# A second recoded weight tile loaded at the entry of the recurrent layer, and one ring of buffers for two kinds of loads

## The chip, the cores and the metric

The kernel runs on one core of one Trainium2 chip. The metric is device time in microseconds (us) of one execution. A core has five engines with an instruction queue each: PE (TensorE, matrix products; PEld is its loading of weights), DVE (VectorE), ACT (ScalarE), POOL (GpSimd) and SP (SyncE, which here only issues DMAs). Each engine takes its instructions in order, and semaphores make one wait for another.

## What is computed

One inference step of two trunk layers on 640 tokens (512 latent tokens, 128 context tokens), 1024 channels, all in f32. Layer 0 is neighbourhood attention and a SwiGLU feed-forward; layer 1 is a gated linear recurrent unit and a SwiGLU feed-forward. The part of the reference at which the change works is the beginning of layer 1:

```
x  = norm(x) * (1 + scale) + shift              # adaLN, needs a sum of squares over all channels
gate, xr = split(x @ w_in)                      # 1024 -> 2 x 1024
xc = depthwise_conv(xr)                         # width 4
r, i = sigmoid(blockdiag(xc) @ w_a + b_a), sigmoid(blockdiag(xc) @ w_i + b_i)   # for two directions
a  = exp(-8 * r * softplus(-lam));  b = sqrt(1 - a*a) * i * xc
h  = scan(a, b) in both directions;  y = (h_fwd + h_bwd) * gelu(gate);  out = y @ w_out
```

## The kernel before

Activations lie with channels on the 128 partitions and tokens along the free axis, so a 1024 x 1024 weight is 64 blocks of 128 x 128; one "tile" holds the 8 blocks that make 128 output channels (512 KB). An f32 product is made of three products of a faster format: weight and activation are each split in a high part and a low part (`hi`, `lo`), and `chunk` adds hi x hi, hi x lo and lo x hi over the 8 blocks: 24 matmuls for 128 output channels and half the tokens (320 columns, or 322 where two extra columns carry the shift of the modulation). `part` does the same for some of the 8 blocks.

**Weight tiles.** `unit` brings a tile in. It is put in one of two kinds of buffers: kind "m" (`whi`, `wlo`, three buffers each, alive for the whole kernel) or kind "x" (`whx`, `wlx`, buffers of the running phase: two in layer 0's feed-forward, three in the recurrent layer). Without a kind named, the units alternate by a running count (`self.nu`). A tile that comes in raw is split by ACT (high part, L1372) and DVE (low part, L1373). Tiles of the recurrent layer and some later ones are recoded ahead: `keep` (L192 to L203) loads the raw tile on POOL's queue into `kraw` (one buffer), ACT and DVE write both parts into `kw` (one buffer, L200 and L201), and POOL stores the 1 MB result in DRAM (L203); `unit` then loads both parts from there on SP's queue (L187), with no work for ACT or DVE. `keep` is called two or three times behind each gate/up pair in the second and third of the three column groups of layer 0's feed-forward: 29 tiles, 16 of `w_in` first.

**Modulation vectors.** `mod_cols` (L263 to L272) computes SiLU(cond) @ w_mod on DVE: a 512 KB tile on POOL's queue into `mraw` (two buffers), then two multiply-and-sum instructions of 128 x 1024 (L271). They are spread over the attention and layer 0's feed-forward.

**Order of work.** A scheduler places the instructions of attention and the feed-forwards in each engine's queue by its own estimate of time; inside `in_order` the engines PE, DVE and ACT keep the order in which the code is written. The recurrent layer, `lru`, is such a part: a table of steps with a lag (`order`, from L1352 on) is run for t = -1, 0, 1, ..., each step for channel tile t + lag.

**The entry.** `project(..., entry=True)` is the last down-projection of layer 0's feed-forward. Behind it `entry` takes tile KT = 8 of `w_in` (the first of `xr`), computes its product for tokens 320 to 639 into bank `p0`, with the first half of the sum of squares' matmuls (`root`, L453) placed in it, and POOL takes the inverse root (L466). In `lru`, step `whole` makes the diagonal of the inverse root on DVE (`diag`, L470), issues the other half of tile 8's product, and spreads the diagonal over all partitions with PE (`spread`, L474); ACT copies the result (L1228). Then `e1` and `e2` scale the product (DVE, L1242), `c1` and `cv` do the convolution (ACT L1260, DVE L1264), and `gates` are matmuls on it (L1273). Between spread and gates PE has `ga` and `gb`: tile 0 of `w_in` (the first of `gate`), 24 matmuls each.

PSUM has eight banks: three `mm`, and five that the running phase names: in layer 0's feed-forward two `at`, one `rr`, two `mx`, in the recurrent layer one `mx` and two double ones, `gp`.

Of the kernel before, what the change touches and what calls it, by code (L numbers as in the profile page):

```python
# [9 lines left out]
F32 = mybir.dt.float32  # L10
# [5 lines left out]
P = 128  # L16
D = 1024
KT = D // P
# [5 lines left out]
CHB = ((320, 642), (0, 320))  # L24
# [16 lines left out]
KH = KT // 2  # L41
# [81 lines left out]
def _pieces(t0, t1):  # L123
    return [(s, max(a, t0), min(b, t1)) for s, a, b in ((0, 0, NLAT), (1, NLAT, NTOK)) if max(a, t0) < min(b, t1)]


class _Step:
    def __init__(self, ctx, nc, tc, i, o):
        self.ctx, self.nc, self.tc, self.i, self.o = ctx, nc, tc, i, o
        self.main = ctx.enter_context(tc.tile_pool(name="main", bufs=1))  # L130
        self.psum = ctx.enter_context(tc.tile_pool(name="psg", bufs=3, space=bass.MemoryType.PSUM))
        self.n, self.ng, self.nu = 0, 0, 0
        self.anchor, self.pbufs, self.lastq, self.whole = None, {}, {}, False

    def nm(self, s):
        self.n += 1
# [55 lines left out]
    def keep(self, todo, n):  # L192
        nc = self.nc
        for _ in range(min(n, len(todo))):
            name, f = key = todo.pop(0)
            raw = self.t([P, KT, P], F32, "kraw", 1, self.sb)
            nc.gpsimd.dma_start(raw, self.i[name][1, f] if name == "gu" else self.i[name][f])
            w = self.t([P, 2, KT, P], F32R, "kw", 1, self.sb)
            with self.tc.issue_after(self.mark):
                nc.scalar.copy(w[:, 0], raw)  # L200
                nc.vector.tensor_tensor(w[:, 1], raw, w[:, 0].bitcast(F32), ALU.subtract)  # L201
            self.kept[key] = d = self.dram.tile([P, 2 * D], F32, tag=f"k{name}{f}", name=f"k{name}{f}")
            nc.gpsimd.dma_start(d, w.rearrange("p h k m -> p (h k m)").bitcast(F32))  # L203
# [59 lines left out]
    def mod_cols(self, l, j, out):  # L263
        nc = self.nc
        for f in range(KT):
            w = self.t([P, D], F32, "mraw", 2, self.sb)
            nc.gpsimd.dma_start(w, self.i["wm"][l * 6 + j - 2, f])  # L267
            for s in range(2):
                prod = self.t([P, D], F32, "mprod", 1, self.sb)
                with self.tc.issue_after(self.anchor) if self.anchor else nullcontext():  # L270
                    nc.vector.scalar_tensor_tensor(prod, w, 1.0, self.csb[:, s], ALU.mult, ALU.mult, accum_out=out[:, s, f:f + 1])  # L271
            yield  # L272
        nc.vector.tensor_tensor(out, out, self.col(f"bm{l}{j}").unsqueeze(1).broadcast_to([P, 2, KT]), ALU.add)
# [221 lines left out]
        return self.stat_spread(self.stat_diag(self.stat_root(t0, t1, newton)))  # L495

    def entry(self, hi, lo):
        self.u0, self.p0 = self.unit(("wi", KT), "m"), self.pg(False)
        t0, t1 = CHB[0]
        ps = self.p0[:, 0:t1 - t0]  # L500
        with self.in_order(ORDERED[:1]):
            self.part(ps, self.u0, hi, lo, range(KT - 1), t0, t1)
            self.rs = self.root(range(0, NTOK, P), [(self.ssq, 0)])
            self.part(ps, self.u0, hi, lo, (KT - 1,), t0, t1)
# [27 lines left out]
    def project(self, w, hi, lo, gk, nxt=None, done=None, ahead=False, entry=False):  # L532
        G = self.need(self.gcols, gk)
        self.whole = entry
        for f in range(KT):
            u = self.unit(w[f], "m" if ahead else None)
            for t0, t1 in CH:
                self.residual(f, t0, t1, self.chunk(u, hi, lo, t0, t1, not ahead or f > 1), G, nxt)
                if nxt:
                    self.scale(f, t0, t1, *nxt)  # L540
            if done:
                done(f)
        if entry:
            self.shift(*nxt)
            self.entry(*nxt[1:])
        elif nxt:
            self.stats()
            self.shift(*nxt)
        self.whole = False
# [489 lines left out]
    def s_sums(self, q):  # L1039
        nc, g = self.nc, q["g"]  # L1040
        q["u"], src = self.t([P, KT, P], F32, "raw", 3), q["u"]
        nc.sync.dma_start(q["u"], src)
        ss = q["S"] = [self.t([P, KT, P], F32, "sum", 2, self.sb) for _ in range(2)]
        s1, s2, s3, s4 = [s[:, a:a + KH] for s in ss for a in (0, KH)]
        g1, g2, u1, u2 = [t[:, a:a + KH] for t in (g, q["u"]) for a in (0, KH)]
        ops = (s1, u1, u2, ALU.add), (s2, s1, g1, ALU.subtract), (s3, g1, u1, ALU.subtract), (s4, g2, s2, ALU.subtract)

        def run(two):
            def go(vector):
                for o in two:  # L1050
                    (nc.vector if vector else nc.gpsimd).tensor_tensor(*o)
            return go
        return run(ops[:2]), run(ops[2:])
# [7 lines left out]
    def sum_weights(self, q):  # L1061
        with self.tc.issue_after(self.pw):
            for run in self.s_sums(q):
                run(False)
        for i in range(2):
            self.s_split(q, i)
# [133 lines left out]
    def lru(self, hi, lo, yhi, ylo, lp):  # L1200
        nc = self.nc
        Z = [{} for _ in range(KT)]

        def tile(shape, tag, bufs):
            return self.t(shape, F32, tag, bufs, lp)
# [13 lines left out]
        def whole(f, z):  # L1219
            if f == 0:  # L1220
                dg = tile([P, NT, P], "gl", 3)
                self.diag(dg, self.rs, NT)
                z["pb"] = self.chunk(z["u"], hi, lo, *CHB[1], False)
                ps = self.pp.tile([P, 1024], F32, tag="gp", name=self.nm("gp"), bufs=2)
                self.spread(dg, range(0, NTOK, P), ps, 0)
                self.rt = self.t([P, NTOK], F32, "r", 1)
                for _, a, b in _pieces(0, NTOK):
                    nc.scalar.copy(self.rt[:, a:b], ps[:, a:b])  # L1228
# [102 lines left out]

        def ga(f, z):
            z["g"] = tile([P, NTOK], "gl", 3)
            z["v"] = self.unit(("wi", f), "x")
            z["pg"] = self.chunk(z["v"], hi, lo, *CHB[0], False)

        def gb(f, z):
            z["ph"] = self.chunk(z["v"], hi, lo, *CHB[1], False)
# [20 lines left out]
        def ls(f, z):  # L1359
            nc.vector.tensor_tensor(ylo[:, f], z["y"], yhi[:, f].bitcast(F32), ALU.subtract)  # L1360

        g, h, e, d = [[fn(n) for n in range(k)] for fn, k in ((gates, 4), (tanhs, 4), (exps, 2), (halves, 2))]
        order = ((g[0], 0), (h[0], 0), (g[1], 0), (h[1], 0), (cl, 0), (e[0], 0), (e[1], 0), (g[2], 0), (xa, 1), (whole, 1), (g[3], 0), (d[0], 0),
                 (h[2], 0), (sc, -1), (su, -1), (e1, 1), (xb, 1), (pad, 1), (h[3], 0), (d[1], 0), (yg, -1), (e2, 1), (egb, 0), (c1, 1),
                 (sq, 0), (ti, 0), (hs, -1), (ga, 1), (cv, 1), (s1, 0), (bg, 1), (ls, -1), (gb, 1), (ega, 1), (ge, 0), (mu, 0))
        for t in range(-1, KT + 1):
            for step, lag in order:
# [27 lines left out]
    def run(self):  # L1395
# [63 lines left out]
            nc.sync.dma_start(o["nv"], V[:, 4])  # L1459
        xhi = self.big(n=NTOK + 2)  # L1460
        xlo = self.big(n=NTOK + 2)
        self.new_x(xpool)
        self.load_x(i["x"])
        xd = dram.tile([D, NTOK], F32, tag="xd", name="xd")
# [45 lines left out]
```

## Time and profile before

| | |
|---|---|
| runs | 1536.15, 1536.77, 1539.8 us (median 1536.77) |
| the profiled execution | 1532.3 us, of which 1530.5 us lie between its first and its last instruction |
| attention, with the start | 0 to about 350 us |
| layer 0, feed-forward with the projection before it | about 350 to 858 us |
| recurrent layer | about 858 to 1020 us |
| its output projection and layer 1's feed-forward | about 1020 to 1530 us |

In the listings, a row of the timeline has the start in us, the time in us, engine, line, operation, tile written <- tiles read, shapes and count; where the engine stood idle ahead of it, brackets give how long and what ended that. Rows of the stages have start and end, length, then busy us and instructions of each engine, the granted PE clock (1.00 is full), the busy share of the 16 DMA engines and GB/s. Matmuls overlap in the records: one of 320 columns is listed with 0.31 us, and the next starts 0.15 us later.

### The profile page before, as it was taken

What the parts mean: (1) busy time and instruction counts of PE and PEld (TensorE: products, weight loads), DVE (VectorE), ACT (ScalarE), POOL (GpSimd) and SP (SyncE); (2) the same over time, 40 slices, a digit from 0 to 9 for tenths busy, and PEclk for the clock granted to TensorE, in tenths of its full rate; (3) what the DMA queues carried; (4) which work ended last, traced back from release to release, by engine and by line L of the source; (5) the groups of instructions that cost most, each with busy time, mean ns of one, the idle gap of its engine ahead of it and who ended that gap; (6) DMA issues with size and microseconds to landing.
All of it is one profiled execution on the core that took longest, in us unless ns stands there. A gap on an engine that the chain in (4) does not pass through costs nothing.

```text
span 1530.5 us, 26161 instructions
## 1 busy us (share of the span) xinstructions
PE 1478.7 (97%) x10295; PEld 1433.8 (94%) x10295; DVE 1075.5 (70%) x2044; ACT 716.9 (47%) x1312; POOL 261.7 (17%) x319
## 2 busy tenths in 40 slices
PE   6999999989999999999999799999999999999997
PEld 4899999879999999999999788889989999999996
DVE  5678788969999997555556368884876666555646
ACT  4676666664333123423344277873644342424342
POOL 2101122100111111110011001112122323232210
PEclk9999999999999999999999899999999999999998
DMA  9545656535566668667668734237333231313111
GB/s 378 165 115 157 182 165 173 149 142 193 179 205 182 202 211 273 210 234 239 222 237 285 279 126 131 88 111 267 112 118 97 69 111 56 111 56 104 62 55 70
DMA packets 80779, 249.61 MB, mean 163 GB/s; under 512 B 9072, under 2 KB 22544, under 8 KB 76816
## 3 DMA queue, kind: packets, MB, share of 16 engines
q1 hardware_dynamic: 59696, 157.59, 31.6%
q0 software_dynamic: 20672, 90.20, 17.9%
q8 instruction: 81, 1.33, 0.3%
q14 instruction: 42, 0.34, 0.1%
q10 hardware_dynamic: 288, 0.16, 0.0%
HBM read 202.02 MB, written 39.33 MB: 158 GB/s over the span
## 4 chain that ended last, share of the span: by engine, by line
PE 88%; DVE 4%; DMA 3%; ACT 2%; issue 1%; POOL 1%; SPq 0%; DVEq 0%; POOLq 0%; ACTq 0%
PE mm L233 13%; PE mm L235 13%; PE mm L234 13%; PE mx L233 5%; PE mx L235 5%; PE mx L234 5%; PE mx L1078 3%; PE mx L1079 3%; PE mx L1080 3%; PE gp L1273 2%; PE op L772 2%; PE tp L696 1%; PE mc L1078 1%; PE mc L1080 1%; PE mc L1079 1%; PE mm L257 1%
## 5 line engine op out<-in xcount | busy, mean ns | idle before, releaser
L234 PE MATMUL mm<-big,whi 128*128 128x320 f32 (+3 forms) x995 | 308.8, 311 | 1.7 <-DVE big L1373 1.6
L233 PE MATMUL mm<-big,whi 128*128 128x320 f32 (+3 forms) x995 | 307.9, 311 | 2.4 <-DVE x L527 1.2
L235 PE MATMUL mm<-big,wlo 128*128 128x320 f32 (+3 forms) x995 | 307.9, 310 | 0.3 <-DVE wlo L1373 0.3
L271 DVE SCALAR_TENSOR_TENSOR mprod<-mraw,csb 128x1024 f32<-128x1024 f32 x160 | 196.1, 1226 | 6.1 <-DMA mraw<-in_wm 5.7
L233 PEld LDWEIGHTS mm<-big,whi 128*128 128x128 f32 x995 | 186.7, 188 | 4.9 <-ACT big L1372 2.1
L234 PEld LDWEIGHTS mm<-big,whi 128*128 128x128 f32 x995 | 187.5, 189 | 3.1 <-DVE big L1373 2.2
L235 PEld LDWEIGHTS mm<-big,wlo 128*128 128x128 f32 x995 | 187.5, 189 | 1.6 <-DVE wlo L1373 0.6
L1372 ACT CAST whi<-raw 128x1024 fp32r<-128x1024 f32 (+2 forms) x107 | 109.5, 1024 | 162.3 <-PE mm L234 101.9
L1373 DVE TENSOR_TENSOR wlo<-raw,whi 128x1024 fp32r<-128x1024 f32 (+2 forms) x107 | 133.3, 1246 | 37.1 <-ACT whi L1372 34.4
L233 PE MATMUL mm<-big,whx 128*128 128x320 f32 (+3 forms) x466 | 145.5, 312 | 7.2 <-DMA whx<-kwi 7.2
L235 PE MATMUL mm<-big,wlx 128*128 128x320 f32 (+3 forms) x466 | 145.5, 312 | 1.0 <-DMA wlx<-kwi 1.0
L234 PE MATMUL mm<-big,whx 128*128 128x320 f32 (+3 forms) x466 | 145.4, 312 | 0.0
L527 DVE SCALAR_TENSOR_TENSOR x<-mm,G,x 128x192 f32<-128x192 f32 (+3 forms) x207 | 83.3, 436 | 73.8 <-PE mm L235 64.0
L267 POOL DMA_DIRECT2D mraw<-in_wm x80 | 43.0, 538 | 371.0 <-DVE mprod L271 262.2
L233 PE MATMUL mx<-big,whi 128*128 128x320 f32 (+2 forms) x325 | 101.6, 313 | 0.0
L234 PE MATMUL mx<-big,whi 128*128 128x320 f32 (+2 forms) x325 | 100.8, 310 | 0.0
L235 PE MATMUL mx<-big,wlo 128*128 128x320 f32 (+2 forms) x325 | 100.8, 310 | 0.0
L233 PEld LDWEIGHTS mm<-big,whx 128*128 128x128 f32 x466 | 88.7, 190 | 7.4 <-DMA whx<-kwi 7.4
L235 PEld LDWEIGHTS mm<-big,wlx 128*128 128x128 f32 x466 | 88.7, 190 | 1.4 <-DMA wlx<-kwi 1.4
L234 PEld LDWEIGHTS mm<-big,whx 128*128 128x128 f32 x466 | 88.8, 191 | 0.0
L1372 ACT CAST whx<-raw 128x1024 fp32r<-128x1024 f32 (+1 forms) x36 | 36.9, 1024 | 71.9 <-PE mm L234 41.1
L235 PE MATMUL mx<-big,wlx 128*128 128x320 f32 (+3 forms) x222 | 69.0, 311 | 0.0
(356 smaller groups left out, 3830.6 us busy)
## 6 DMA issues: line engine op xcount, KB each, us to landing
raw<-in_gu SPq DMA_DIRECT2D x84, 512.0 KB, 3.6
mraw<-in_wm POOLq DMA_DIRECT2D x80, 512.0 KB, 3.9
kwi<-kw POOLq DMA_DIRECT2D x16, 1024.0 KB, 5.2
raw<-in_dn SPq DMA_DIRECT2D x24, 512.0 KB, 3.6
sw<-in_wm SPq DMA_DIRECT2D x16, 512.0 KB, 10.1
raw<-in_wqk SPq DMA_DIRECT2D x16, 512.0 KB, 4.2
kraw<-in_wi POOLq DMA_DIRECT2D x16, 512.0 KB, 6.0
kwlo<-kw POOLq DMA_DIRECT2D x8, 1024.0 KB, 5.2
```

Of the source, the lines that this page charges most:

```text
L233: nc.tensor.matmul(ps, hi[:, k], xhi[:, k, s], start=(k == 0), stop=False)
L234: nc.tensor.matmul(ps, hi[:, k], xlo[:, k, s], start=False, stop=False)
L235: nc.tensor.matmul(ps, lo[:, k], xhi[:, k, s], start=False, stop=(k == nk - 1))
L267: nc.gpsimd.dma_start(w, self.i["wm"][l * 6 + j - 2, f])
L271: nc.vector.scalar_tensor_tensor(prod, w, 1.0, self.csb[:, s], ALU.mult, ALU.mult, accum_out=out[:, s, f:f + 1])
L527: last = self.nc.vector.scalar_tensor_tensor(xs, ps[:, a - t0:b - t0], G[:, s, f:f + 1], xs, ALU.mult, ALU.add).ins
L772: mm = nc.tensor.matmul(out, v, w, start=start, stop=stop)
L1078: nc.tensor.matmul(ps, hi[:, k], xh[:, k], start=start and k == 0, stop=False, skip_group_check=not start)
L1079: nc.tensor.matmul(ps, hi[:, k], xl[:, k], start=False, stop=False, skip_group_check=not start)
L1080: nc.tensor.matmul(ps, lo[:, k], xh[:, k], start=False, stop=(k == KH - 1), skip_group_check=not start)
L1372: self.nc.scalar.copy(hi, v)
L1373: return self.nc.vector.tensor_tensor(lo, v, hi.bitcast(F32), ALU.subtract).ins
```

## The change

Four edits:

1. `entry` also takes tile 0 of `w_in`, into a buffer of kind "m", at once behind tile 8 (it was taken by step `ga`, into kind "x").
2. The first half of tile 0's product (blocks 0 to 3, tokens 320 to 639) is issued ahead of the spread, into the phase's bank `mx`; the second half (blocks 4 to 7) stands where the whole product stood. Tile 1 is taken in the same place, in kind "x"; step `ga` takes tiles itself from tile 2 on.
3. In the last down-projection of layer 0's feed-forward the kind alternates by the tile's own number instead of the running count.
4. `kraw` is gone: in layer 0's feed-forward `keep` and `mod_cols` share one ring `mraw` of three buffers (before: one and two). In the attention `mod_cols` has two, as before.

```
         for _ in range(min(n, len(todo))):
             name, f = key = todo.pop(0)
-            raw = self.t([P, KT, P], F32, "kraw", 1, self.sb)
+            raw = self.t([P, D], F32, "mraw", 3, self.sb).rearrange("p (k m) -> p k m", k=KT)
...
-            w = self.t([P, D], F32, "mraw", 2, self.sb)
+            w = self.t([P, D], F32, "mraw", self.nraw, self.sb)
...
     def entry(self, hi, lo):
-        self.u0, self.p0 = self.unit(("wi", KT), "m"), self.pg(False)
+        self.u0, self.v0, self.p0 = self.unit(("wi", KT), "m"), self.unit(("wi", 0), "m"), self.pg(False)
...
-            u = self.unit(w[f], "m" if ahead else None)
+            u = self.unit(w[f], "m" if ahead else "mx"[f % 2] if entry else None)
...
                 z["pb"] = self.chunk(z["u"], hi, lo, *CHB[1], False)
+                z["pg"] = self.ps("mx")[:, 0:CHB[0][1] - CHB[0][0]]
+                Z[1]["v"] = self.unit(("wi", 1), "x")
+                self.part(z["pg"], self.v0, hi, lo, range(KH), *CHB[0])
                 ps = self.pp.tile([P, 1024], F32, tag="gp", name=self.nm("gp"), bufs=2)
                 self.spread(dg, range(0, NTOK, P), ps, 0)
...
         def ga(f, z):
             z["g"] = tile([P, NTOK], "gl", 3)
-            z["v"] = self.unit(("wi", f), "x")
-            z["pg"] = self.chunk(z["v"], hi, lo, *CHB[0], False)
+            if f > 1:
+                z["v"] = self.unit(("wi", f), "x")
+            if f:
+                z["pg"] = self.chunk(z["v"], hi, lo, *CHB[0], False)
+            else:
+                z["v"] = self.v0
+                self.part(z["pg"], z["v"], hi, lo, range(KH, KT), *CHB[0])
```

`self.nraw` is 2 at the start and set to 3 ahead of the feed-forward. How the queues change at three places:

SP at the end of layer 0's feed-forward; `kwi_6528` is the recoded tile 8 of `w_in`, 6687 tile 9, 6846 tile 10, 7005 tile 11, and 6535 and 6694 are tiles 0 and 1; `xd` is the store of the residual stream, `gw` the small gate weights. Before:

```order
222 L187 DMA whi_9787<-kwi_6687 128x1024
223 L187 DMA wlo_9788<-kwi_6687 128x1024
224 L1471 DMA xd<-x_4084 128x640 x2
225 L187 DMA whi_9951<-kwi_6846 128x1024
226 L187 DMA wlo_9952<-kwi_6846 128x1024
227 L1471 DMA xd<-x_4084 128x640 x2
228 L187 DMA whi_10127<-kwi_7005 128x1024
229 L187 DMA wlo_10128<-kwi_7005 128x1024
230 L1215 DMA gw_9656<-in_wg 128x512
231 L187 DMA whx_9711<-kwi_6535 128x1024
232 L187 DMA wlx_9712<-kwi_6535 128x1024
```

The same stretch of SP with the change:

```order
222 L187 DMA whi_9609<-kwi_6535 128x1024
223 L187 DMA wlo_9610<-kwi_6535 128x1024
224 L1480 DMA xd<-x_4084 128x640 x2
225 L187 DMA whi_9791<-kwi_6687 128x1024
226 L187 DMA wlo_9792<-kwi_6687 128x1024
227 L1480 DMA xd<-x_4084 128x640 x2
228 L1215 DMA gw_9660<-in_wg 128x512
229 L187 DMA whx_9692<-kwi_6694 128x1024
230 L187 DMA wlx_9693<-kwi_6694 128x1024
```

Tile 0 stands where tile 9 stood, tile 9 where tile 10 stood, and tiles 10 and 11 come behind tiles 1 and 2.

PE at the entry of the recurrent layer; `mm_9662` is the second half of tile 8's product, `gp_9687` the spread, `mm_9715` the first product of tile 0. Before:

```order
5380 L233 MATMUL mm_9662<-big_9076,whi_9605 128x320
5381 L234 MATMUL mm_9662<-big_9077,whi_9605 128x320
5382 L235 MATMUL mm_9662<-big_9076,wlo_9606 128x320
5383 L474 MATMUL gp_9687<-gl_9660,ones_72 128x128 x5
5384 L233 MATMUL mm_9715<-big_9076,whx_9711 128x322
```

With the change (`mm_9666` is tile 8's product now, `gp_9708` the spread, and `mx_9691` the first product of tile 0, of which the 12 matmuls 5383 to 5394 stand ahead of the spread and 12 behind):

```order
5381 L234 MATMUL mm_9666<-big_9077,whi_9605 128x320
5382 L235 MATMUL mm_9666<-big_9076,wlo_9606 128x320
5383 L242 MATMUL mx_9691<-big_9076,whi_9609 128x322
5384 L243 MATMUL mx_9691<-big_9077,whi_9609 128x322
...
5394 L244 MATMUL mx_9691<-big_9076,wlo_9610 128x322
5395 L474 MATMUL gp_9708<-gl_9664,ones_72 128x128 x5
5396 L242 MATMUL mx_9691<-big_9076,whi_9609 128x322
```

The number of matmuls is the same; half of tile 0's first product has moved across the spread.

POOL in the last column group of layer 0's feed-forward (`kwlo` and `kgu` are stores of recoded tiles, `in_wm` loads of `mod_cols`, `rs` the inverse root). Before:

```order
183 L197 DMA kraw_8915<-in_gu 128x1024
184 L203 DMA kgu_8920<-kw_8917 128x2048
185 L197 DMA kraw_8922<-in_gu 128x1024
186 L203 DMA kgu_8927<-kw_8924 128x2048
187 L197 DMA kraw_9062<-in_gu 128x1024
188 L203 DMA kgu_9067<-kw_9064 128x2048
189 L197 DMA kraw_9069<-in_gu 128x1024
190 L466 TENSOR_TENSOR rs_9639<-var_9637,mhalf_68 128x5
191 L203 DMA kgu_9074<-kw_9071 128x2048
```

With the change:

```order
180 L267 DMA mraw_8781<-in_wm 128x1024
181 L203 DMA kwlo_8766<-kw_8763 128x2048
182 L197 DMA mraw_8915<-in_gu 128x1024
183 L197 DMA mraw_8922<-in_gu 128x1024
184 L203 DMA kgu_8773<-kw_8770 128x2048
185 L197 DMA mraw_9062<-in_gu 128x1024
186 L203 DMA kgu_8920<-kw_8917 128x2048
187 L197 DMA mraw_9069<-in_gu 128x1024
188 L203 DMA kgu_8927<-kw_8924 128x2048
189 L203 DMA kgu_9067<-kw_9064 128x2048
190 L203 DMA kgu_9074<-kw_9071 128x2048
191 L466 TENSOR_TENSOR rs_9643<-var_9641,mhalf_68 128x5
```

Raw loads stand up to two stores ahead of their own, loads of `mod_cols` stand among them until the third column group, and the last store stands ahead of the inverse root. On DVE the last low part of a recoded tile (L201) stood between the variance and the diagonal; with the change the last of them stands 32 instructions ahead of the variance. In the feed-forward, two L201 and three or four L271 stand in most gate/up pairs of the second and third column groups, where before there were mostly one or two L201 alone (the L271 lay in the first group, its projection and the first pairs of the second).

More of the change, by code (lines that the diff above doesn't have):

```diff
@@ L132, in __init__ @@
         self.n, self.ng, self.nu = 0, 0, 0
-        self.anchor, self.pbufs, self.lastq, self.whole = None, {}, {}, False
+        self.anchor, self.pbufs, self.lastq, self.whole, self.nraw = None, {}, {}, False, 2
     def nm(self, s):
@@ L1461, in run @@
         xlo = self.big(n=NTOK + 2)
+        self.nraw = 3
         self.new_x(xpool)
```

## The prediction

> **What bounds the kernel now.** I read the page, then PE's waits, then the stages around the largest of them.
>
> ```profile
> PE 1478.7 (97%) x10295; PEld 1433.8 (94%) x10295; DVE 1075.5 (70%) x2044; ACT 716.9 (47%) x1312; POOL 261.7 (17%) x319
> ```
>
> PE is busy for 97% of the span. A change can only win where PE stands still or runs slowly. PE's waits between 780 and 900 us:
>
> ```profile
> PE mm L233 <- DMA whx<-kwi: 7.2, 1, 7.2
> PE gp L474 <- DVE gl L470: 1.9, 1, 1.9
> PE mm L235 <- DMA wlx<-kwi: 1.0, 1, 1.0
> ```
>
> These three lie at the entry of the recurrent layer. The stages (busy us of PE and PEld first, then the rest, the clock, DMA share and GB/s):
>
> ```profile
> 400.00:470.00 70.00, 70.00 (x474) 70.00 (x473) 67.18 (x125) 22.16 (x44) 8.45 (x16) 1.00 0.61 201
> 600.00:700.00 100.00, 100.00 (x678) 100.00 (x677) 53.16 (x82) 33.64 (x50) 10.55 (x20) 1.00 0.67 224
> 838.00:850.00 12.00, 12.00 (x84) 12.00 (x83) 8.09 (x17) 5.46 (x12) 1.06 (x2) 1.00 0.88 302
> 860.00:870.00 10.00, 2.26 (x12) 1.69 (x12) 4.14 (x9) 2.33 (x8) 0.22 (x1) 0.57 0.97 355
> 883.00:1020.00 137.00, 134.38 (x809) 120.28 (x808) 108.92 (x161) 108.88 (x167) 15.85 (x14) 1.00 0.30 100
> ```
>
> Before the entry PE has no gap, in the recurrent layer 2.6 us of 137; between them it nearly stops while the DMA engines run full. A matmul of 320 columns costs 100 us / 678 = 0.1475 us. PE's timeline there:
>
> ```profile
> 857.99 0.31 PE L235 MATMUL mm<-big,wlo 128*128 128x320 f32 x1
> 860.20 1.35 PE L474 MATMUL gp<-gl,ones 128*128 128x128 f32 x10 [1.90 <-DVE gl L470]
> 868.80 0.64 PE L233 MATMUL mm<-big,whx 128*128 128x322 f32 x1 [7.25 <-DMA whx<-kwi]
> 870.70 0.63 PE L235 MATMUL mm<-big,wlx 128*128 128x322 f32 x1 [0.99 <-DMA wlx<-kwi]
> 874.89 0.43 PE L235 MATMUL mm<-big,wlx 128*128 128x322 f32 x1
> 879.59 0.59 PE L1273 MATMUL gp<-xc,gw 128*128 128x512 f32 x1
> ```
>
> From 858.14 (one step after the last matmul of tile 8) to the first gate matmul at 879.59 are 21.45 us. The work in it is the spread, 1.35, and tile 0's 48 matmuls, 48 x 0.1475 = 7.08: together 8.43. So 13.0 us are lost: 1.90 + 7.25 + 0.99 of waiting, and about 2.7 because PE ran at half its clock, as the stages cut at the clock's steps show:
>
> ```profile
> 858.08:861.49 3.41, 1.51 (x12) 1.19 (x10) 1.96 (x2) 0.03 (x1) 0.60 (x1) 1.00 0.60 150
> 861.49:864.90 3.41, 0.06 (x1) 0.00 (x0) 1.42 (x5) 2.30 (x8) 0.00 (x0) 0.50 0.94 339
> 864.90:868.32 3.42, 0.00 (x0) 0.00 (x0) 2.66 (x3) 0.02 (x1) 0.00 (x0) 0.50 1.01 413
> 871.73:875.14 3.41, 3.41 (x14) 3.41 (x14) 0.00 (x0) 0.00 (x0) 0.00 (x0) 0.50 0.91 370
> 1015.07:1018.49 3.42, 2.06 (x8) 0.98 (x6) 3.42 (x7) 3.41 (x5) 1.05 (x2) 1.00 0.00 0
> ```
>
> A stretch with 1.51 us busy of 3.41 is followed by half clock, one with 2.06 of 3.42 is not.
>
> **The change part by part.** *Tile 0 comes early.* SP's queue, and the time from issue to landing in the stretch from 560 to 860 us:
>
> ```profile
> 831.42 0.32 SPq L187 DMA_DIRECT2D whi<-kwi  x1
> 843.79 0.32 SPq L187 DMA_DIRECT2D whi<-kwi  x1
> 859.63 0.33 SPq L187 DMA_DIRECT2D whx<-kwi  x1
> ...
> kwi<-kw POOLq DMA_DIRECT2D x16, 1024.0 KB, 5.2
> kgu<-kw POOLq DMA_DIRECT2D x5, 1024.0 KB, 6.1
> xd<-x SPq DMA_DIRECT2D x8, 320.0 KB, 6.2
> wlo<-kwi SPq DMA_DIRECT2D x4, 512.0 KB, 7.6
> whx<-kwi SPq DMA_DIRECT2D x1, 512.0 KB, 9.1
> ```
>
> Tile 0 was issued at 859.63, behind tile 11, and took 9.1 us. Now it takes the place of tile 9 at 831.42 (that buffer comes free then), its low part a little later, and lands by 831.8 + 1.4 + 7.6 = 841, 17 us ahead of its use. The 7.25 and 0.99 go. What is moved for it: tile 9 goes to 843.8 and lands by 853, needed behind the first three gates at about 871. Tile 1 stands behind the stores of the residual stream, the last of which (issue 851.7) must land first, 851.7 + 6.2 = 858; with 9.1 for itself it is there at 867, needed at about 879. Tile 10 needs tile 8's buffer, free at 858, and has until about 888. These moves cost nothing; the cover of the tightest is 12 us.
>
> *Half of tile 0's product ahead of the spread.* 12 x 0.1475 = 1.77 us of work from 858.14 to 859.91. Does the diagonal come in time?
>
> ```profile
> 855.88 1.19 POOL L466 TENSOR_TENSOR rs<-var,mhalf 128x5 f32<-128x5 f32 x1 [4.66 <-DVE var L456]
> ...
> 857.01 1.05 ACT L200 CAST kw<-kraw 128x1024 fp32r<-128x1024 f32 x1 [4.80 <-DMA kraw<-in_gu]
> 861.59 0.75 ACT L1228 COPY r<-gp 128x512 f32<-128x512 f32 x2 [3.48 <-PE gp L474]
> ...
> 858.09 1.23 DVE L201 TENSOR_TENSOR kw<-kraw,kw 128x1024 fp32r<-128x1024 f32 x1 [2.36 <-ACT kw L200]
> 859.24 0.82 DVE L470 TENSOR_TENSOR gl<-ident,rs 128x640 f32<-128x640 f32 x1
> 862.21 0.60 DVE L1242 TENSOR_TENSOR xr<-mm,r 128x192 f32<-128x192 f32 x2 [2.15 <-ACT r L1228]
> 864.96 2.73 DVE L1264 SCALAR_TENSOR_TENSOR xc<-xr,cols,xc 128x643 f32<-128x643 f32 x3 [1.33 <-ACT xc L1260]
> ```
>
> The inverse root was ready at 857.07, but the diagonal stood behind the last recoded tile's low part, which waited for ACT and that for a raw load. With the change this L201 stands 32 instructions earlier; the diagonal runs from 857.1 to 857.9 and no longer holds PE. Spread: 859.91 to 861.26, 0.29 earlier than now.
>
> *What is late next.* From the spread's end to the end of the convolution it was 867.69 - 861.55 = 6.14 us, a chain of ACT and DVE that the change doesn't touch. So the convolution ends at 861.26 + 6.14 = 867.40. PE has 36 matmuls of tile 0 left behind the spread, 5.31 us, until 866.57, then waits 0.9 for the convolution. First gate at 867.5 in place of 879.59: a gain of 12.1 us, of at most 13.0. The bank `mx`, which tile 9's product needs next, is read out by DVE directly behind the convolution, at about 867.9, and needed at 871.
>
> *Clock.* A stretch of 3.41 us with a gap of 0.9 is at least 2.5 busy, more than the 2.06 that kept the full clock, so I cost it at nothing; were it dropped once, 3.41 us at half rate lose 1.7. The Trainium skill (TensorE: Matmul & The Clock Gate, "What's actually happening") has the clock fall after an idle window of about 3.4 us. In this trace it fell after a window that was 44% busy, with no gap over 1.90 us: by the page's rule the 0.9 us are far from it, by the trace they are nearer, but on the safe side.
>
> *Kinds in turn.* The order of PE shows `whi` for even and `whx` for odd tiles of this projection with and without the edit: nothing.
>
> *One ring of three.* The work stays; its place changes. L271 move from the first column group (DVE 67.18 of 70 us busy, PE without a gap) to the second and third, where DVE had 53 of 100. By the order, a gate/up pair (96 matmuls, 14.2 us) then has up to two recoded tiles and two tiles of L271. I cost that at nothing, because PE can run about four banks, 4 x 24 x 0.1475 = 14 us, ahead of DVE; a gain is excluded, since PE has no gap there. The other end is the second rival.
>
> Later parts keep their order but for the names of banks and the order of two products at the end: 0, at most 0.5 us either way (my estimate from the products' 12 x 0.1475 = 1.8 us).
>
> **Sum.** Profiled execution 1532.3 - 12.1 = 1520.2 us. That execution is 4.5 us below the median of the runs, 1536.77; from the median it is 1524.7 us.
>
> **Rivals.** *1. The entry loses part of it* (14%): the clock falls once more (1.7), tile 1 or 9 lands late, or the convolution ends some us later because ACT and DVE aren't free. For it: 355 GB/s behind 860 us, and a new order of loads. Against: the covers above. Gain 5 to 10, about 1529.
>
> *2. Recoding becomes the bound of the feed-forward, slower than before* (8%). One buffer `kw` must be stored before the next tile is written. Its period:
>
> ```profile
> 779.60 0.54 POOL L203 DMA_DIRECT2D kwlo<-kw  x1 [9.02 <-DVE kw L201]
> ```
>
> Issue 0.54 + landing 5.2 to 6.1 + ACT 1.05 + DVE 1.23 = 8.0 to 8.9 us. Two in a pair need 16.0 to 17.8 us, and the pair has 14.2: 1.8 to 3.6 late. By the order eight pairs have two. If nothing is absorbed, that is 14 to 29 us, and the kernel takes 1539 to 1554. It decides from 12 us on. For it: ACT waits up to 4.8 us for a raw load now. Against: those waits cost PE nothing; the pairs between them and the projections have one or none, and 29 tiles x 8.9 = 258 us fit in the 290 us from the first to the last.
>
> *3. It ends even* (14%): half of rival 2, lateness of 8 to 16 us that PE sees, through the DMA. A pair with two recoded tiles and two of L271 moves 2 x 0.52 + 2 x 1.57 + 2 x 0.52 = 5.2 MB in 14.2 us, 369 GB/s; the 12 us ahead of 850 ran at 302 GB/s with a share of 0.88, hence about 340 when full. Then such a pair takes 15.4 us, 1.2 more; with eight, and the store's lateness added in part, 10 us. About 1535. The Trainium skill (DMA: Bandwidth & Descriptors, "Specifications") gives about 358 GB/s from HBM for a core, by which such a pair takes 14.6 us and eight lose 3.5 us, 1528. The trace shows 413 GB/s in one stretch of 3.4 us, so it doesn't hold as a ceiling there.
>
> *4. The ring or tile 0's early load isn't what the code says*: excluded by the order, which shows both.
>
> **Numbers.** My forecast has 64%. A difference of 0.3%, 4.6 us, is about what a measurement of this kernel can tell. Faster by more: the forecast and rival 1, 0.78; the same: rival 3, 0.14; slower: rival 2, 0.08. The range runs from 1519 (the profiled execution less 13.0) to 1536 (no gain): it leaves out rival 2, part of rival 3, and little below.
>
> **What would show it.** Right: in the changed profile no wait of PE on `whx<-kwi` or `gl` at the entry, the clock full there, the first gate matmul 9 to 10 us behind the last of tile 8 in place of 21, behind a wait below 1.5 us for `xc`; no gap of PE from 400 to 858. Wrong: PE waiting on DVE or ACT in the feed-forward's second and third groups (L201, L271 or L200 waiting on DMA ahead of them), the entry beginning later than 858; or a wait on tile 9 or 1 in the recurrent layer.

## The result and the profile after

The changed kernel takes 1526.9 us (median of 10 runs, 1522.86 to 1531.98) against 1536.82 us (10 runs, 1535.65 to 1539.8): a ratio of 0.9936, 95% interval 0.9923 to 0.9949, so 9.9 us less. The forecast was 1524.7 in a range of 1519 to 1536, and faster. The profiled execution takes 1526.2 us with a span of 1524.4, 6.1 less than before.

Line 1 of the page:

```profile
PE 1480.3 (97%) x10295; PEld 1434.0 (94%) x10295; DVE 1073.8 (70%) x2044; ACT 715.9 (47%) x1312; POOL 258.8 (17%) x319
```

The share of each engine is as before. What changed is where PE stands. Its waits between 392 and 1060 us:

```profile
PE mx L233 <- ACT big L1380: 1.6, 1, 1.6
PE mx L242 <- issue: 1.1, 1, 1.1
PE gp L1276 <- issue: 1.0, 1, 1.0
PE mm L243 <- DVE big L1368: 0.5, 1, 0.5
PE mm L233 <- ACT big L1380: 0.4, 1, 0.4
```

The waits on tile 0 and on the diagonal are gone. Two on a cast of ACT are new, at the ends of column groups, where there was none; the one of 1.0 is the forecast wait for the convolution. PE at the entry (the last matmul of tile 8, the spread, the first gates), and DVE there:

```profile
862.61 0.31 PE L235 MATMUL mm<-big,wlo 128*128 128x320 f32 x1
...
864.54 1.28 PE L474 MATMUL gp<-gl,ones 128*128 128x128 f32 x10
...
872.12 3.62 PE L1276 MATMUL gp<-xc,gw 128*128 128x512 f32 x12 [0.96 <-issue]
```

```profile
861.73 0.83 DVE L470 TENSOR_TENSOR gl<-ident,rs 128x640 f32<-128x640 f32 x1 [1.38 <-POOL rs L466]
...
869.28 2.73 DVE L1267 SCALAR_TENSOR_TENSOR xc<-xr,cols,xc 128x643 f32<-128x643 f32 x3 [1.33 <-ACT bias L1209]
```

The first gate comes 872.12 - 862.76 = 9.36 us behind tile 8 (before 21.45; forecast 867.5 - 858.14 = 9.36), 0.11 behind the convolution's end at 872.01. But the diagonal is ready at 862.56, before tile 8 ends, and the spread starts only at 864.54: the half product stands in its way.

The clock in the stretch with that wait, and a stretch of the feed-forward cut at the same place in both kernels, first after, then before:

```profile
869.52:872.93 3.41, 2.45 (x14) 1.86 (x13) 2.83 (x4) 0.00 (x0) 0.00 (x0) 1.00 0.70 253
```

```profile
475.00:575.00 100.00, 100.00 (x679) 100.00 (x678) 41.01 (x68) 22.06 (x36) 1.59 (x3) 1.00 0.27 85
575.00:810.00 235.00, 233.84 (x1577) 233.32 (x1575) 188.11 (x319) 86.82 (x147) 40.79 (x77) 1.00 0.87 300
```

```profile
475.00:575.00 100.00, 100.00 (x679) 100.00 (x678) 93.41 (x170) 21.53 (x36) 13.72 (x26) 1.00 0.64 203
575.00:810.00 235.00, 235.00 (x1588) 235.00 (x1587) 136.54 (x220) 88.58 (x151) 25.33 (x48) 1.00 0.69 235
```

The third figure is DVE. The ring has moved some 52 us of its work out of the first stretch into the second, where the recoded tiles are, and the DMA share there went from 0.69 to 0.87. PE loses 1.2 us in it (and 0.8 just behind).

**Stages.** PE runs 10295 matmuls in every kernel here, so the same places are found by counting them in order of start: the 2901st (in the feed-forward's first projection), the 6051st (the last of tile 8), the first gate, the 7301st (in the output projection of the recurrent layer). The table has, from the profiled executions, the start of the 2901st; from there to the start of the 6051st; from 0.15 behind that to the first gate; from there to the 7301st; and from that to the end of the span. E1 to E12 are the experiments below. Ratios are those to the kernel before, with 95% intervals.

| kernel | ratio | ahead | feed-forward | entry | layer | rest |
|---|---|---|---|---|---|---|
| before | 1 | 392.4 | 465.61 | 21.44 | 194.6 | 456.4 |
| changed | 0.9936 [0.9923, 0.9949] | 394.4 | 468.18 | 9.35 | 194.3 | 458.0 |
| E1 no ring | 0.9928 [0.9913, 0.9943] | 398.3 | 465.61 | 10.37 | 194.2 | 457.7 |
| E2 ring alone | 0.9932 [0.9910, 0.9955] | 394.7 | 468.32 | 8.22 | 194.6 | 456.5 |
| E3 early tile alone | 1.0010 [0.9997, 1.0024] | 396.7 | 465.61 | 10.21 | 206.4 | 457.1 |
| E4 no half ahead | 0.9938 [0.9916, 0.9961] | 395.5 | 468.13 | 8.26 | 194.4 | 456.2 |
| E5 order alone | 0.9913 [0.9898, 0.9929] | 393.4 | 465.61 | 10.71 | 194.5 | 454.3 |
| E6 early tile, tile 1 | 0.9944 [0.9932, 0.9955] | 393.6 | 465.61 | 13.31 | 196.2 | 456.8 |
| E7 changed, halves | 0.9926 [0.9910, 0.9941] | 391.8 | 465.64 | 9.37 | 194.4 | 458.6 |
| E8 E4, halves | 0.9904 [0.9887, 0.9921] | 397.7 | 467.16 | 8.24 | 194.4 | 456.0 |
| E9 E2, halves | 0.9922 [0.9907, 0.9936] | 396.7 | 468.22 | 8.23 | 195.9 | 456.3 |
| E10 E5, halves | 0.9967 [0.9952, 0.9982] | 394.8 | 477.66 | 8.22 | 196.1 | 455.6 |
| E11 no turn | 0.9948 [0.9928, 0.9968] | 397.3 | 469.90 | 9.35 | 196.7 | 457.8 |
| E12 order, recoded earlier | 0.9911 [0.9893, 0.9928] | 395.7 | 465.64 | 8.56 | 196.1 | 458.3 |

The profiled execution's 6.1 us are: entry -12.09, layer -0.22, feed-forward +2.57, ahead +2.06, rest +1.59. Ahead of the 2901st matmul PE's instructions are the same; of the others, the ring takes one raw load and one copy of a recoded tile (ACT, at 343.16 us before) out of this stage. Kernels that run the same instructions there still differ by up to 5.9 us (before and E1), and the changed kernel and E11, which is its program throughout, by 2.8. So single sums tell little below 3 us, the middle three columns tell more. What scatters in the outer ones is mostly half clock, by the stretches that each profile lists; the changed kernel's profile has three behind its first 30 us that the one of before has not:

```profile
169.81:173.22 3.41, 3.41 (x15) 3.41 (x14) 3.17 (x6) 1.49 (x4) 0.00 (x0) 0.51 0.25 99
384.85:388.26 3.41, 3.41 (x14) 3.41 (x14) 2.31 (x7) 0.00 (x0) 2.83 (x3) 0.51 0.13 49
1504.42:1507.83 3.41, 3.41 (x18) 3.41 (x17) 1.14 (x2) 0.00 (x0) 0.00 (x0) 0.51 0.13 42
```

Each costs up to 1.7 us; E11's profile has others (two behind 298.8 us, one behind 1036.1).

### The profile page after: what moved, and what is told of

It reads as the page before. It is cut to its first block, busy times and chain, and to the rows that moved or that the text cites. A ratio compares the mean times of both kernels' runs of the same rounds, so it can differ in the third digit from the quotient of the medians.

```text
span 1524.4 us, 26130 instructions
## 1 busy us (share of the span) xinstructions
PE 1480.3 (97%) x10295; PEld 1434.0 (94%) x10295; DVE 1073.8 (70%) x2044; ACT 715.9 (47%) x1312; POOL 258.8 (17%) x319
## 5 line engine op out<-in xcount | busy, mean ns | idle before, releaser
L233 PE MATMUL mm<-big,whi 128*128 128x320 f32 (+2 forms) x1003 | 311.5, 313 | 2.7 <-ACT big L1380 1.5
L234 PE MATMUL mm<-big,whi 128*128 128x320 f32 (+2 forms) x1003 | 312.7, 312 | 1.3 <-DVE big L1381 1.2
L235 PE MATMUL mm<-big,wlo 128*128 128x320 f32 (+2 forms) x1003 | 311.8, 311 | 0.0
L271 DVE SCALAR_TENSOR_TENSOR mprod<-mraw,csb 128x1024 f32<-128x1024 f32 x160 | 195.6, 1223 | 8.6 <-DMA mraw<-in_wm 8.3
L233 PEld LDWEIGHTS mm<-big,whi 128*128 128x128 f32 x1003 | 189.4, 189 | 5.7 <-ACT big L1380 2.7
L234 PEld LDWEIGHTS mm<-big,whi 128*128 128x128 f32 x1003 | 190.2, 190 | 2.7 <-DVE big L1381 1.9
L234 PE MATMUL mm<-big,whx 128*128 128x320 f32 (+3 forms) x450 | 139.6, 310 | 0.0
L235 PE MATMUL mm<-big,wlx 128*128 128x320 f32 (+3 forms) x450 | 139.6, 310 | 0.0
L233 PE MATMUL mm<-big,whx 128*128 128x320 f32 (+3 forms) x450 | 139.4, 310 | 0.0
L234 PEld LDWEIGHTS mm<-big,whx 128*128 128x128 f32 x450 | 85.0, 189 | 0.0
L235 PEld LDWEIGHTS mm<-big,wlx 128*128 128x128 f32 x450 | 84.9, 189 | 0.0
L233 PEld LDWEIGHTS mm<-big,whx 128*128 128x128 f32 x450 | 84.9, 189 | 0.0
L234 PE MATMUL mx<-big,whx 128*128 128x320 f32 (+3 forms) x222 | 68.9, 310 | 0.0
```

The source lines that it names most:

```text
L233: nc.tensor.matmul(ps, hi[:, k], xhi[:, k, s], start=(k == 0), stop=False)
L234: nc.tensor.matmul(ps, hi[:, k], xlo[:, k, s], start=False, stop=False)
L235: nc.tensor.matmul(ps, lo[:, k], xhi[:, k, s], start=False, stop=(k == nk - 1))
```

## The experiments

Theory A, that of the prediction with the profile after beside it: the gain is the early tile's, and the ring costs. Each part was taken away or made alone.

**E1, the ring undone.**

```
-            raw = self.t([P, D], F32, "mraw", 3, self.sb).rearrange("p (k m) -> p k m", k=KT)
+            raw = self.t([P, KT, P], F32, "kraw", 1, self.sb)
...
-        self.nraw = 3
```

> The changed kernel with the raw tiles as before (kraw one buffer, mraw two), so the shared ring is undone and the early tile, the product ahead of the spread and the turn of kinds stay. Theory A (the entry gives all the gain, the ring costs PE about 2.0 us in the feed-forward and is not needed for the gain): no wait of PE between 400 and 850 us, where the changed kernel has 0.44 and 1.55; the diagonal comes 1.9 us behind tile 8's last matmul and PE waits 0.1 to 0.4 us for it; first gate 9.4 to 9.8 us behind tile 8's end (changed kernel 9.36). About 1.7 us less than the changed kernel: ratio to before near 0.9925. Rival B (the two waits are not the ring's but come by chance or from the loads): both waits stay, the time is that of the changed kernel or more, 0.9936 to 0.995. Rival C (without the ring the diagonal holds the spread): 1.5 us or more of waiting ahead of the spread.

PE has no wait in the feed-forward, 465.61 as before: the 2.57 us are the ring's. In the entry it waits 0.79 us for the diagonal, more than expected, and the first gate comes 1.0 us later than in the changed kernel. By these two stages E1 takes 1.6 us less; the ratios can't be told apart. Theory A holds for the feed-forward.

**E2, the ring alone**, on the kernel before.

> The kernel before with the shared ring of three raw tiles alone. Theory A: one or two waits of PE on a cast of ACT in the second and third groups, 1 to 3 us together; at the entry the diagonal is ready when tile 8 ends, but PE then waits some 9 us for tile 0 in place of 1.9 + 7.25, so that the entry gains less than 0.5; ratio 1.0005 to 1.002. Rival B: no waits in the feed-forward, ratio 1.000. Rival D (the diagonal was a part of the gain): the entry is 1.5 us or more shorter, ratio 0.999.

Theory A falls, and the entry gains far more than the 1.5 us of rival D. The kernel with nothing but the ring is as fast as the changed one, and its entry is shorter, 8.22. PE's waits from 392 to 1060 us, and PE and SP at the entry:

```profile
PE mx L242 <- ACT lt L1283: 2.6, 1, 2.6
PE mx L233 <- ACT big L1372: 1.4, 1, 1.4
PE mm L233 <- ACT big L1372: 0.7, 1, 0.7
```

```profile
863.06 0.31 PE L235 MATMUL mm<-big,wlo 128*128 128x320 f32 x1
863.20 1.29 PE L474 MATMUL gp<-gl,ones 128*128 128x128 f32 x10
...
871.43 3.54 PE L1273 MATMUL gp<-xc,gw 128*128 128x512 f32 x12
```

```profile
858.18 0.32 SPq L187 DMA_DIRECT2D whx<-kwi  x1
...
863.25 0.32 SPq L187 DMA_DIRECT2D whi<-kwi  x1
```

Tile 0, still of kind "x" and not taken early, is issued 5.0 us ahead of tile 8's end (863.21), not 1.5 behind it. In SP's queue of the kernel before, tile 11 (`whi_10127`) stands ahead of the gate weights and of tile 0 (`whx_9711`). Tile 11 needs tile 8's buffer, so its load waits for tile 8's last matmul, which ended at 858.14 there, and tile 0 behind it waits as well:

```profile
858.19 0.32 SPq L187 DMA_DIRECT2D whi<-kwi  x1
...
859.63 0.33 SPq L187 DMA_DIRECT2D whx<-kwi  x1
```

With the ring the scheduler, which places SP's instructions by its own estimate of time, puts them the other way round:

```
228 L1215 DMA gw_9656<-in_wg 128x512
229 L187 DMA whx_9711<-kwi_6535 128x1024
...
236 L187 DMA whi_10127<-kwi_7005 128x1024
```

**E3, the early tile alone**, on the kernel before.

```
-        self.u0, self.p0 = self.unit(("wi", KT), "m"), self.pg(False)
+        self.u0, self.v0, self.p0 = self.unit(("wi", KT), "m"), self.unit(("wi", 0), "m"), self.pg(False)
...
-            z["v"] = self.unit(("wi", f), "x")
+            z["v"] = self.unit(("wi", f), "x") if f else self.v0
```

> The kernel before with tile 0 loaded early into the other kind, and nothing else: its product stands whole behind the spread. Theory A: no wait on the tile's load; PE waits 1.9 us for the diagonal, spreads for 1.35 and runs 7.08 of tile 0, so that the first gate starts 10.4 to 10.8 us behind tile 8's end (before 21.45); ratio near 0.993. Rival E (the early half is what counts, and the load alone only shifts the wait): first gate 13 us or more behind tile 8's end, ratio above 0.995.

The entry is close to what was expected, 10.21; the time, which was to fall to a ratio near 0.993, is that of before or a little more. PE's waits from 392 to 1060 us:

```profile
PE mm L242 <- DVE x L527: 7.5, 1, 7.5
PE mx L242 <- ACT lt L1283: 2.6, 1, 2.6
PE gp L474 <- DVE gl L470: 1.7, 1, 1.7
```

All is given back at the opening of layer 1's feed-forward: 7.5 us of waiting for the residual stream, 10.24 us of half clock from 1036.4 us on, the stage 11.8 us longer. SP's waits in 1000 to 1045 us begin so, here and in the kernel before:

```profile
SPq L187 <- DVE big L1360: 30.1, 1, 30.1
```

```profile
SPq L187 <- DVE lt L1307: 18.6, 1, 18.6
```

The first weight tile of kind "x" of the next phase waits for L1360, the last step of the recurrent layer, where it waited for an earlier one, and the residual stream's loads stand behind it.

**E4, the changed kernel with tile 0's product whole behind the spread.**

```
-                self.part(z["pg"], self.v0, hi, lo, range(KH), *CHB[0])
...
-                self.part(z["pg"], z["v"], hi, lo, range(KH, KT), *CHB[0])
+                self.part(z["pg"], z["v"], hi, lo, range(KT), *CHB[0])
```

> The changed kernel with tile 0's product whole behind the spread (bank, early tile and ring kept). Theory A: the diagonal is ready 0.2 us ahead of tile 8's end, so the spread starts at once, the convolution ends 7.5 us behind tile 8 while PE is busy for 8.4 with spread and product: no wait on the convolution (0.96 in the changed kernel), first gate 8.4 to 8.7 us behind tile 8's end; 0.7 to 1.0 us less than the changed kernel. Rival F (the half covers the diagonal): PE waits 1 us or more ahead of the spread and the first gate starts 9.4 us or more behind tile 8's end.

The entry is 8.26, a little shorter than expected, with no wait on the convolution: the half costs 1.09 us where the diagonal is in time. The median itself can't tell 1 us.

**E5, the order of SP's queue alone**, on the kernel before.

```
-            with self.in_order():
+            with self.in_order(ORDERED + (mybir.EngineType.SP,)):
```

> The kernel before with the recurrent layer's DMAs held to the order of the code on SP's queue, so that tile 0's load stands directly behind the stores of the residual stream, ahead of tiles 9, 10 and 11; raw tiles, kinds and banks are as before. Theory G (in the kernel before, tile 0's load waited in the queue behind tile 11's, which waits for PE to finish tile 8; the shared ring gains because it moves tile 0's load ahead of it): tile 0's load is issued well ahead of tile 8's last matmul, the 7.25 us wait falls below 2, and the entry is 7 us or more shorter; in the layer other waits may come, because the gate tiles' loads now hold the queue. Rival H (tile 0's place in memory is the last raw tile's, so its load cannot start before that is recoded): it is issued at or behind the last low part of a recoded tile, 1 us or more behind tile 8's last matmul, and the wait stays at 6 to 9 us.

SP, and the last low part of a recoded tile on DVE:

```profile
857.75 0.32 SPq L187 DMA_DIRECT2D whx<-kwi  x1
```

```profile
857.85 1.23 DVE L201 TENSOR_TENSOR kw<-kraw,kw 128x1024 fp32r<-128x1024 f32 x1 [1.06 <-ACT kw L200]
858.99 0.82 DVE L470 TENSOR_TENSOR gl<-ident,rs 128x640 f32<-128x640 f32 x1
```

Theory G holds and rival H falls: tile 0's load goes out 1.45 us ahead of tile 8's end (859.20) and before the raw tile is read for the last time. The waits on it are 0.4 and 0.7 us in place of 7.2 and 1.0, that on the diagonal 0.6 in place of 1.9. A queue's order, with no buffer, kind or bank changed, gives 10.7 of the 12.1 us, and costs nothing in the feed-forward.

**E6, the early tile with tile 1 asked for ahead of the spread.**

```
+                Z[1]["v"] = self.unit(("wi", 1), "x")
                 ps = self.pp.tile([P, 1024], F32, tag="gp", name=self.nm("gp"), bufs=2)
...
-            z["v"] = self.unit(("wi", f), "x")
+            if f == 0:
+                z["v"] = self.v0
+            elif f > 1:
+                z["v"] = self.unit(("wi", f), "x")
```

> The kernel before with tile 0 early, and tile 1's load written ahead of the spread as in the change; product whole behind the spread, no ring. Theory I (the early tile alone gave its 10.8 us back because the x tiles were then first asked for later, got other places in memory, and the first tiles of the next layer had to wait for the last step of the recurrent layer; asked for early they do not): the wait of 7.5 us at the next layer's opening and the half clock around it are gone, the load that waited 30 us is issued some 10 us earlier relative to the layer's end, the entry is as with the early tile alone (first gate 10.4 to 10.8 us behind tile 8's end); ratio 0.993. Rival J (what came late there was the residual stream's load, pushed by an earlier layer on a full queue): the wait stays at 5 us or more, ratio 1.000.

Theory I holds for the waits: none at the opening, layer 196.2, ratio 0.9944 where E3 has 1.0010. The load that went out at 1026.79 in E3 goes out at 1003.55 here, 13 us earlier when each is counted from its layer stage's end:

```profile
1003.55 0.32 SPq L187 DMA_DIRECT2D whx<-kwlo  x1
```

So this line of the second edit keeps the first edit's gain from being lost. The entry, 13.31, is longer than expected: 3.4 us of waiting for the diagonal in this profile, then half clock.

**E7, E8, E9, recoded tiles stored by halves**: in the changed kernel, in E4 and in E2.

```
-            w = self.t([P, 2, KT, P], F32R, "kw", 1, self.sb)
+            w, v = [self.t([P, KT, P], F32R, t, 1, self.sb) for t in ("kwh", "kwl")]
...
-            nc.gpsimd.dma_start(d, w.rearrange("p h k m -> p (h k m)").bitcast(F32))
+            for h, q in enumerate((w, v)):
+                nc.gpsimd.dma_start(d[:, h * D:h * D + D], q.rearrange("p k m -> p (k m)").bitcast(F32))
```

> The changed kernel with the recoded tile in two buffers of half the size, each stored by itself as soon as it is written (two stores of 512 KB for one of 1 MB). Theory K (PE's waits of 0.44 and 1.55 us in the feed-forward come from ACT's copy of a recoded tile, which waits for the store of the one before and holds the cast that PE needs): both waits are gone, about 2.0 us less than the changed kernel, ratio near 0.9925. Rival L (they come from DVE's or the DMA engines' load): they stay or move, same time as the changed kernel within 0.5 us.

> The changed kernel with stores by halves and tile 0's product whole behind the spread. By theory A and K together: no wait in the feed-forward, first gate 8.2 to 8.5 us behind tile 8's end, 2.5 to 3.0 us less than the changed kernel, ratio near 0.992. If K is wrong: 0.9 less, from the entry alone.

> The kernel before with two things only: the shared ring, and recoded tiles stored by halves; tile 0's load, its kind, its bank and its place behind the spread are as before. If the early tile, the half ahead of the spread and the turn of kinds add nothing once the ring is there: feed-forward within 1.6 us of the kernel before (465.6 us from the first products of its first projection to tile 8's last matmul), first gate 8.1 to 8.4 us behind tile 8's end, ratio 0.990 to 0.992, as the changed kernel with halves and the whole product. If they add something beside the ring: an entry of 9 us or more, or a wait on tile 0's load, ratio above 0.993.

The wait that was to go, in the changed kernel: ACT, DVE and PE at 807 to 811 us.

```profile
807.53 1.05 ACT L200 CAST kw<-mraw 128x1024 fp32r<-128x1024 f32 x1 [2.56 <-DMA kgu<-kw]
...
810.33 0.46 ACT L1380 CAST big<-sg 128x320 fp32r<-128x320 f32 x1 [0.80 <-DVE sg L810]
```

```profile
808.61 1.23 DVE L201 TENSOR_TENSOR kw<-mraw,kw 128x1024 fp32r<-128x1024 f32 x1 [2.71 <-ACT kw L200]
809.75 0.54 DVE L810 SCALAR_TENSOR_TENSOR sg<-up,bias,sg 128x320 f32<-128x320 f32 x1
```

```profile
810.84 0.41 PE L233 MATMUL mx<-big,whi 128*128 128x320 f32 x1 [1.55 <-ACT big L1380]
```

The copy (L200) waits for the store of the tile before; the low part (L201) waits for the copy; the last step of the last up product (L810) stands behind the low part; PE needs its cast at the beginning of the down-projection. The order on ACT matters as well. In the kernel before, the copy stands behind both casts of a column group's last pair, and it waits for a raw load, not for a store:

```profile
801.80 0.46 ACT L1372 CAST big<-sg 128x320 fp32r<-128x320 f32 x1 [0.21 <-DVE sg L810]
804.39 1.05 ACT L200 CAST kw<-kraw 128x1024 fp32r<-128x1024 f32 x1 [2.13 <-DMA kraw<-in_wlo]
```

So the ring did two things there: it brought the raw tile earlier, so that the store became what the copy waits for, and it moved the copy ahead of the last cast. E12 below also has the copy ahead of the last cast, without a wait of PE; the order alone does not make the wait.

In E7 both waits are gone, 465.64. But E8 and E9 run the same feed-forward and have one each at 663 us, of 0.95 and 2.06 us, on DVE, so that E9's feed-forward misses what was expected of it. E9's row is

```profile
PE mm L235 <- DVE big L1374: 2.1, 1, 2.1
```

There the low part waits for the store of the previous tile's low half. With the ring, the three profiles of halves have 465.64, 467.16 and 468.22, the four of whole stores 468.18, 468.32, 468.13 and 469.90. Whether halves gain something is open. Between 560 and 862 us ACT's copies wait 30 us for stores in E7, where they waited 61 in the changed kernel, and DVE's low parts wait 14, where they waited for none: a part of the wait has moved. E9's entry of 8.23 repeats E2's: beside the ring, the early tile, the half and the turn add nothing.

**E10, halves with E5; E12, E5 with the last tile recoded one place earlier.** E12's edit beside E5's:

```
-                if ci:
-                    self.keep(todo, 3 if j == n - 1 else 2)
+                if ci or j == n - 1:
+                    self.keep(todo, (3 if j == n - 1 else 2) if ci else 1)
```

> The kernel before with the layer's loads held to the order of the code, and recoded tiles stored by halves; one raw tile as before, no ring, no early tile. If the place in SP's queue is all that the entry lacked, and the diagonal is late only because the last recoded tile waited for a store of 1 MB: feed-forward 465.6, entry 8.2 to 9.6, ratio 0.989 to 0.991, the fastest of all. If the last recoded tile is late for another reason (its raw load): the wait for the diagonal stays at 0.5 to 2 us and the entry at 9.8 to 11, ratio as with the order alone, 0.9913.

> The kernel before with the layer's loads held to the order of the code, and one tile recoded at the end of the first column group, so that the list is done one tile earlier and the last low part stands ahead of the variance on DVE; raw tiles, kinds and banks as before, no ring, no early tile. If the place in SP's queue and the last recoded tile are all that the entry lacked: no wait on the diagonal, tile 0's load issued 4 us or more ahead of tile 8's end, first gate 8.1 to 8.6 us behind it (10.7 with the order alone, 9.35 in the changed kernel), feed-forward 465.6 us, ratio 0.988 to 0.991. If the tile recoded in the first group collides there: waits of PE behind 392 us and a feed-forward of 467 us or more; if tile 0's place in memory still holds its load: a wait of 0.5 us or more on it.

E10, expected to be the fastest, is not: its entry is 8.22, but its feed-forward 477.66, 12 us longer. PE's waits there from 392 to 1000 us:

```profile
PE mm L234 <- ACT big L1373: 5.8, 2, 3.6
PE mx L243 <- ACT lt L1284: 2.6, 1, 2.6
PE mm L235 <- DVE big L1374: 0.8, 1, 0.8
```

These lie at the ends of column groups again, and 10.2 us of half clock behind them cost about 5 more. ACT's copies wait 96 us for raw loads between 560 and 862 us, where they wait 34 in E5, and at 658.13 one that waited 6.38 stands ahead of both casts of the last pair; in E5 it stands behind both. So recoding can hold the feed-forward up after all. E5 shows that one raw tile alone does not do it, E7 to E9 that halves with the ring do not cost this much; how much is the place of the copy was not tried. E12 has no wait but one of 2.62 in the layer, feed-forward 465.64 and entry 8.56, together 3.3 us less than the changed kernel. Its load of tile 0 goes out 3.4 us ahead of tile 8's end, not the 4 or more expected, and its ratio is just above the expected range.

**E11, the changed kernel without the turn of kinds**, the same program on every engine.

> The changed kernel without the turn of kinds in the last projection. Its instructions stand in the same order with the same buffers on every engine, so every theory expects the time of the changed kernel; it measures how far two sets of runs of one program lie apart, and which of the half-clock stretches outside the entry come by chance. Feed-forward 468.0 to 468.4, entry 9.3 to 9.4, ratio 0.9925 to 0.9945.

It takes 1529.5 us, where the changed kernel had 1526.9. The feed-forward, 469.90, is longer than expected: the wait of 1.55 us at the third column group's end is 3.15 here. So two sets of runs of one program lie 2.6 us apart by their medians and 1.8 by their ratios, and the ring's cost in the feed-forward is 2.5 to 4.3 us over the four profiles with whole stores.

E5, E8 and E12 have the lowest ratios (0.9904 to 0.9913). E8's interval ends below where those of the changed kernel's program begin (0.9923 and 0.9928); those of E5 and E12 overlap with them.

## Why the prediction was right, and where it was not

- **The bound and the size**: right. The entry, 12.1 us forecast, gave 12.09, with the forecast wait for the convolution (0.9; 0.96) and full clock in its stretch, of which 2.45 us were busy ("at least 2.5").
- **"Tile 0 comes early ... The 7.25 and 0.99 go"**: the waits went, but the cause was over-named. Two edits each take them away: E2 has the ring alone and E3 the early tile alone. E5 shows the step that both have in common, tile 0's place in SP's queue. The prediction quoted that queue ("behind tile 11") and worked out the new order for the four edits together; it did not ask what the ring alone does to it.
- **"Half of tile 0's product ahead of the spread"**: put down as a spread 0.29 us earlier, it loses 1.1 us (E4). The prediction had both numbers: diagonal ready at 857.9, tile 8 done at 858.14. With these the spread needs no cover, and product and spread together end 8.43 us behind tile 8, not 9.36.
- **"I cost that at nothing, because PE can run about four banks ... ahead of DVE"**: this step failed. It holds inside a column group. At its end the projection needs the group's last pair at once, and both waits are there, 0.44 and 1.55 us; they are the sign of being wrong that the prediction itself names. So the second and third rivals were right in their mechanism (a store of `kw` holds ACT, and DVE behind it) and too large in their size: 2.5 to 4.3 us, not 8 and more, since PE sees the lateness in two places and not in eight pairs.
- **"Kinds in turn: nothing"**: right; E11 has the same program. **Later parts, at most 0.5 either way**: the layer's stage gives 0.22. The rest's 1.59 has a stretch of half clock in it.
- **The median**: 1526.9 for 1524.7. The ring's cost, left out of the sum, is as large as what is missing; two sets of one program differ by as much. The profiled execution took 1526.2 us for 1520.2: 2.6 of that are the feed-forward's and 3.7 the two outer stages', where half clock scatters.

The early tile's give-back (E3) was on no list. The change avoids it by the line tested in E6; why an earlier request for the buffer changes what the next phase waits for was read from who is waited for, and the places in memory themselves were not looked at.

## What to carry to other kernels

Read a late load by what stands ahead of it in its queue before giving it another buffer: here one line that keeps the queue in order gave at least as much as four edits. When two edits remove the same wait, time each alone; a second remedy, left in, may only cost. A buffer of slack covers a late engine inside a loop, and not at the loop's end, where the next stage needs the last result at once.

## What the runs showed of the hardware

Whether the clock falls behind a wait depends on where the wait lies in the stretches of 3.41 us at whose ends the clock changes in these traces. The same wait of 2.62 us at the recurrent layer's end, in E5 and in E12, each with the stretch that holds most of it:

```profile
1005.80:1009.21 3.41, 1.67 (x7) 0.79 (x5) 3.41 (x6) 3.40 (x5) 1.44 (x2) 1.00 0.00 0
```

```profile
1008.32:1011.73 3.41, 1.50 (x10) 1.50 (x11) 3.38 (x8) 3.39 (x5) 1.36 (x2) 1.00 0.02 5
1011.73:1015.15 3.42, 3.42 (x15) 3.42 (x14) 2.58 (x3) 3.39 (x4) 0.00 (x0) 0.50 0.33 79
```

With 1.67 us of PE's 3.41 busy the next stretch had the full clock, with 1.50 it had half, and the layer took 1.5 us more. This wait is in eight profiles: with 0.79 to 1.50 us busy (E3, E6, E9, E10, E12) the clock fell, with 1.67 to 2.06 (before, E2, E5) it did not. These figures are no limit for other places: in E11 a stretch with 1.52 us busy (from 810.72) was followed by the full clock, in the changed kernel one with 1.88 (from 166.40) by half. The stretch ahead of 384.85 us in the changed kernel was busy throughout and was followed by half clock too; 24 matmuls of a single column start in it, the first of them here:

```profile
382.16 1.39 PE L453 MATMUL at<-ones,ssq 128*128 128x1 f32 x12
```

So time listed as busy alone does not settle it, and what does stays open. The Trainium skill (TensorE: Matmul & The Clock Gate, "What's actually happening") has the fall after an idle window of this length; none of the stretches named in this section was idle throughout.
